# A two-layer hybrid transformer on one core: the low part of the score products over 128 rows, and a softmax tile's transpositions, scores and values each in one run

## The chip, the cores and the metric

The kernel runs on 1 of the 8 cores of one Trainium2 chip. A core has TensorE (PE: matrix products; its weight loads are shown apart as PEld), VectorE (DVE), ScalarE (ACT), GpSimd (POOL) and SyncE (SP), which here issues the DMAs. The metric is the time of one execution on the device in microseconds (us). Before the change the median of 3 runs is 3375.31 us.

## The reference

Two layers work on 1024 latent tokens and 256 context tokens of width 1024. In each layer one input projection feeds three groups of heads: gated linear attention, neighbourhood attention on a 16 x 64 grid (6 heads), and sliding-window attention (6 query heads, 2 key heads). An output projection and a SwiGLU feed-forward block follow. The change concerns the two softmax groups:

```
# neighbourhood attention: 8 x 32 keys around a block of queries, with a bias, and all context keys
s_loc = jnp.einsum('brnqhd,brnkchd->bhrnqkc', q_blk, k_blk) * scale + bias
s_ctx = jnp.einsum('brnqhd,blhd->bhrnql', q_blk, kc) * scale
p = jax.nn.softmax(jnp.concatenate([s_loc, s_ctx], axis=-1), axis=-1)
o = einsum(p_loc, v_blk) + einsum(p_ctx, vc)
# sliding window: 3 blocks of 128 keys, all context keys, and one sink logit for each head
p = jax.nn.softmax(jnp.concatenate([s_loc, s_ctx, s_sink], axis=-1), axis=-1)[without the sink]
o = einsum(p_loc, vb) + einsum(p_ctx, vc)
```

In the first layer the context tokens are queries too, over the context keys alone.

## The kernel before, in words

All work is in fp32. For products that need more exactness, an operand is split into a high part, rounded to the fast format fp32r, and a low part, the rest. The big projections take three fp32r products for each pair of operands (high x high, high x low, low x high).

**Softmax tiles.** A tile is 128 queries of two heads ("pair"). A head has 64 channels, so the scores have 64 rows to sum over. `make_q` (L785) loads the high part of a head's queries into rows 0 to 63 and the low part into rows 64 to 127. `make_k` (L791) loads the high part of the keys into both halves of k1, and the low part into rows 0 to 63 of k2 alone. `qk` (L798) adds two products in one PSUM bank: all 128 rows of q with k1 (L799: high x high plus low x high), and 64 rows of q with k2 (L800: high x low). q is the stationary operand and is loaded for every product.

`softmax_pair` (L803) makes the scores of a tile: for each head a product pair with the 256 context keys (bank sc) and one with up to 384 local keys (bank sl). DVE evicts both into the tile P and takes the extreme of each row (L809 for sc, L815 for sl, whose custom instruction also adds the bias or the mask); ACT then takes the exponential and its row sums in place (L819). `pv_pair` (L831) makes the values. P has up to five chunks of 128 keys. For two chunks at a time, four PE transpositions (two chunks, two heads; L838) fill a bank ptp, which DVE (first two chunks, L844) or ACT (the others, L842) copies to a buffer pT. Then four products (L847) of 128 rows and 64 columns add to the output, where each head takes one half of the columns of PE. `normalised` (L853) follows after the last tile of a group of up to four: reciprocal of the sums, copied 64 wide (bc, L865), transposed on PE (rrt, L869), evicted by ACT (ys, L875) and multiplied with the output (L876), which SP then stores.

**Order.** `pipeline` (L880) sets the order in which the code issues this: the scores of a tile, then the values of the tile before it (depth 1). A scheduler then places the instructions of each engine by priority and by a timeline of its own; each engine runs its list strictly in that order. Buffers come from pools that rotate: PSUM banks in three pools (p_a 2, p_b 3, p_c 3; sc and sl are in p_c), six buffers w2 for pT, bc and ys, and for P four buffers p5 in the sliding window and four each of wh and wl in neighbourhood attention.

**Stages.** In layer 0 the sliding window (swa) is interleaved with the last projections (nqk, nvp) and with the modulation vectors for later (bank mod, L301, weights wm by DMA). Neighbourhood attention (na) follows: three pairs of heads, each with loads of q, k1, k2, values (vw) and bias tables (gt, gm; POOL adds them, L1022), and with two halves of four tiles. Layer 0 has 30 tiles in each group, layer 1 has 24. The output projection (op) and the feed-forward block (pg, pu, pd) come after.

Of the kernel before, what the change touches and what calls it, by code (L numbers as in the profile page):

```python
# [11 lines left out]
F32 = mybir.dt.float32  # L12
# [3 lines left out]
ALU = mybir.AluOpType  # L16
# [71 lines left out]
def hybrid_layers(ctx: ExitStack, tc: tile.TileContext, A, K, out):  # L88
    nc = tc.nc
    V, S, G, PE, SY = nc.vector, nc.scalar, nc.gpsimd, nc.tensor, nc.sync  # L90
# [36 lines left out]
    def p_b(s):  # L127
        return ps.tile([128, 512], F32, tag="pb", name=nm(s), bufs=3)
# [10 lines left out]
    def small(s, w=1):  # L139
        return sm.tile([128, w], F32, tag=f"s{w}", name=nm(s), bufs=7)  # L140
# [53 lines left out]
    yD = [[dr.tile([D, n], F32, name=f"yD{l}_{o}") for (o, n) in (B0, B1, BC)] for l in range(DEPTH)]  # L194
# [61 lines left out]
    def rev(t, off, dims):  # L256
        return bass.AP(tensor=t.tensor, offset=t.offset + off, ap=[list(t.ap[0])] + dims)
# [527 lines left out]
    def make_q(src, r0, nn, alloc):  # L785
        q = alloc("q", F32R)
        for i in range(2):
            SY.dma_start(q[64 * i:64 * i + 64, 0:nn].bitcast(F32), src[i][r0:r0 + 64, 0:nn])
        return q

    def make_k(src, r0, alloc):  # L791
        k1, k2 = alloc("k1", F32R), alloc("k2", F32R)
        for i in range(2):
            SY.dma_start(k1[64 * i:64 * i + 64].bitcast(F32), src[0][r0:r0 + 64, :])
        SY.dma_start(k2[0:64].bitcast(F32), src[1][r0:r0 + 64, :])
        return k1, k2

    def qk(dst, q, k, qs, ks):  # L798
        PE.matmul(dst, qs(q), ks(k[0]), start=True, stop=False)  # L799
        PE.matmul(dst, qs(q)[0:64], ks(k[1])[0:64], start=False, stop=True)  # L800


    def softmax_pair(nl, emit_loc, emit_ctx, bias, nsk, m, sums):  # L803
# [24 lines left out]
        else:  # L828
            S.activation(dst, src, AF.Copy)

    def pv_pair(pr, nck, vfun, op, bank):  # L831
        c = 0
        while c < nck:
            w = min(2, nck - c)
            tp = bank("ptp")
            for cc in range(w):
                for i in range(2):
                    PE.transpose(tp[:, (cc * 2 + i) * 128:(cc * 2 + i + 1) * 128],  # L838
                                 pr[i][:, (c + cc) * 128:(c + cc + 1) * 128], ident)
            pT = t_w2("pT")  # L840
            if c >= 2:
                S.activation(pT[:, :w * 256], tp[:, :w * 256], AF.Copy)  # L842
            else:
                V.tensor_copy(pT[:, :w * 256], tp[:, :w * 256])  # L844
            for cc in range(w):
                for i in range(2):
                    PE.matmul(op[64 * i:64 * i + 64], vfun(i, c + cc),  # L847
                              pT[:, (cc * 2 + i) * 128:(cc * 2 + i + 1) * 128],
                              start=(c + cc == 0), stop=(c + cc == nck - 1), tile_position=(0, 64 * i))
            c += w  # L850


    def normalised(op, mins, sums, nt, nsk=None, grid=False):  # L853
        bc = t_w2("bc")
        n = 128 * nt
        rr = small("rr", 8)
        if nsk is not None:
            e = small("e", 8)
            V.tensor_tensor(e[:, :2 * nt].rearrange("p (j h) -> p j h", h=2),
                            mins[:, :2 * nt].rearrange("p (j h) -> p j h", h=2),  # L860
                            nsk.unsqueeze(1).to_broadcast([128, nt, 2]), ALU.subtract)
            S.activation(e[:, :2 * nt], e[:, :2 * nt], AF.Exp)
            V.tensor_tensor(sums[:, :2 * nt], sums[:, :2 * nt], e[:, :2 * nt], ALU.add)
        V.reciprocal(rr[:, :2 * nt], sums[:, :2 * nt])
        V.tensor_copy(bc[:, :n].rearrange("p (j c) -> p j c", c=64),  # L865
                      rr[:, :2 * nt].unsqueeze(2).to_broadcast([128, 2 * nt, 64]))
        rt = p_b("rrt")
        for j in range(nt):
            PE.transpose(rt[:, 128 * j:128 * j + 128], bc[:, 128 * j:128 * j + 128], ident)  # L869
        ys = t_w2("ys")  # L870
        dst, num, den = ys[:, :n], op[:, :n], rt[:, :n]
        if grid:
            dst = dst.rearrange("p (r n c) -> p r n c", n=4, c=16)
            num, den = [t.rearrange("p (n r c) -> p r n c", r=8, c=16) for t in (num, den)]
        S.activation(dst, den, AF.Copy)  # L875
        V.tensor_tensor(dst, dst, num, ALU.mult)  # L876
        return ys


    def pipeline(tiles, depth):  # L880
        late = []
        for scores, values in tiles:
            scores()
            late.append(values)
            if len(late) > depth:
                late.pop(0)()
            yield
        for values in late:
            values()

    def swa_mix(l, ctx_out):
        nn = N if ctx_out else T
        vsw = t_s("vsw")
        SY.dma_start(vsw.rearrange("p (t e) -> p t e", e=128), vswD[l].rearrange("(t p) e -> p t e", p=128))
        ks = [make_k(swD[l][2 * g + 1], 64, t_s) for g in range(2)]

        def tile(pair, qs, nsk, b, i, jt, nt, box):
            lo, hi = (max(i - 1, 0), min(i + 2, 8)) if i < 8 else (0, 0)
            m0 = 128 * (lo - i + 1) if i < 8 else 0
            cks = list(range(lo, hi)) + [8, 9]  # L900
            nl = 128 * (hi - lo)

            def qsl(x):
                return x[:, i * 128:(i + 1) * 128]

            def scores():
                if jt == 0:
                    box["m"], box["sums"] = small("m", 8), small("sums", 8)
                box[jt] = softmax_pair(
                    nl,  # L910
                    lambda a, dst: qk(dst, qs[a], ks[pair[a][0]], qsl, lambda x: x[:, lo * 128:hi * 128]),
                    lambda a, dst: qk(dst, qs[a], ks[pair[a][0]], qsl, lambda x: x[:, T:N]),
                    lambda a: swam[:, m0:m0 + nl], nsk,
                    box["m"][:, 2 * jt:2 * jt + 2], box["sums"][:, 2 * jt:2 * jt + 2])

            def vf(a, c):
                o = cks[c] * 128 + 64 * pair[a][0]
                return vsw[:, o:o + 64]

            def values():  # L920
                if jt == 0:
                    box["op"] = p_b("swo")
                op = box["op"]
                pv_pair(box[jt], len(cks), vf, op[:, 128 * jt:128 * jt + 128], p_b)
                if jt == nt - 1:
                    ys = normalised(op, box["m"], box["sums"], nt, nsk)
                    for a in range(2):
                        r0 = 640 + 64 * (3 * pair[a][0] + pair[a][1])
                        SY.dma_start(yD[l][b][r0:r0 + 64, :], ys[64 * a:64 * a + 64, :128 * nt])
            return scores, values  # L930
# [10 lines left out]
        return pipeline(tiles(), 1)  # L941

    CS = (0, 8, 24, 32)
    PAT = (0, 1, 1, 2)
# [2 lines left out]
    def na_mix(l, ctx_out):  # L947
# [4 lines left out]
        def tile(p, qs, ks, half, n, nt, gms, vw, box):  # L952
            ctx_tile = half == 2
# [18 lines left out]
            def vf(a, c):  # L972
# [3 lines left out]
                o = (c if ctx_tile else c - 3) * 384 + 128 * p + 64 * a  # L976
                return vctx[:, o:o + 64]

            def values():
                if n == 0:  # L980
                    box["op"] = p_b("nao")
                op = box["op"]
                pv_pair(box[n], 2 if ctx_tile else 5, vf, op[:, n * 128:(n + 1) * 128],
                        p_a)
                if n == nt - 1:
                    ys = normalised(op, box["m"], box["sums"], nt, grid=not ctx_tile)
                    SY.dma_start(yD[l][half][256 + 128 * p:384 + 128 * p, :], ys[:, :128 * nt])
            return scores, values

        def tiles():  # L990
            for p in range(3):
# [22 lines left out]
                for half in range(2):  # L1014
# [13 lines left out]
        return pipeline(tiles(), 1)  # L1028


    def out_proj(l, blks):
# [218 lines left out]
```

## Time and profile before

| what | value |
|---|---|
| median of 3 runs | 3375.31 us (3372.78 to 3394.1) |
| the profiled execution | 3358.87 us; its span 3357.1 us |
| TensorE clock granted, mean | 0.98 |
| read from HBM, written | 251.25 MB, 60.91 MB |
| instructions | 49501 |

The profile shows one execution. Its sums give the busy time of each engine, with PE busy 97% of the span; the chain is the work that ended last, followed back from the end. A group of instructions is shown by line, engine, operation and the names of what it writes and reads (`sc<-k,q`), with its shape: `64*128 64x256` is a stationary operand of 64 rows and 128 columns, and 256 columns that move past it. An fp32 product whose operands aren't in the fast format is shown as two matmuls (so four value products of a chunk pair appear as x8). The ends of matmuls are modelled, so the time that one costs is read from its start to the start of the next. Durations in a group's row are in ns, window bounds in us from the start of the span.

### The profile page before, as it was taken

To read this page: it belongs to the slowest core of one execution; us is meant where nothing else is said; L and a number is where in the kernel's file an instruction comes from. 1 tells how busy PE (TensorE), PEld (TensorE's weight loads), DVE (VectorE), ACT (ScalarE), POOL (GpSimd) and SP (SyncE) were. 2 spreads that over 40 slices of the span, in tenths; PEclk is the share of its full clock that TensorE was granted. 3 is DMA by queue.
4 is the path that set the end of the run, shared out by engine and by line. 5 is a ranking of instruction groups with operands and counts; after the bars stand their busy time and mean duration, and the time that the engine had idled before them with its cause. 6 is when DMAs were issued, how large, how long until landed. Compare 5 with 4: busy or idle time off the path is not lost.

```text
span 3357.1 us, 49501 instructions
## 1 busy us (share of the span) xinstructions
PE 3262.3 (97%) x19732; PEld 2668.1 (79%) x19732; DVE 1821.2 (54%) x3585; ACT 931.1 (28%) x1738; POOL 756.6 (23%) x633
## 2 busy tenths in 40 slices
PE   7999999999999999999999899999999999999998
PEld 5888876667888888888888798876668788888887
DVE  3255444556576666666556635435556555555555
ACT  4332133455321111111112332224554211111112
POOL 1011100120179889885000101010211000000000
PEclk9999999999999999999999998999999999999999
DMA  7243447454222222221111223344444111111111
GB/s 245 77 150 104 130 134 191 136 150 143 88 66 76 82 76 82 79 76 59 43 38 33 85 90 110 111 135 122 130 129 139 51 48 47 51 45 51 51 51 57
DMA packets 316208, 315.39 MB, mean 94 GB/s; under 512 B 62445, under 2 KB 246473, under 8 KB 315977
## 3 DMA queue, kind: packets, MB, share of 16 engines
q1 hardware_dynamic: 314824, 308.04, 30.4%
q10 hardware_dynamic: 1152, 4.19, 0.3%
q8 instruction: 155, 2.54, 0.3%
q14 instruction: 77, 0.62, 0.1%
HBM read 251.25 MB, written 60.91 MB: 93 GB/s over the span
## 4 chain that ended last, share of the span: by engine, by line
PE 92%; DVE 3%; DMA 2%; ACT 1%; issue 1%; POOL 0%; SPq 0%; ACTq 0%; DVEq 0%; POOLq 0%
PE pg L432 16%; PE pd L1093 16%; PE pu L432 16%; PE op L432 6%; PE nqk L432 5%; PE gp L432 5%; PE ptp L838 4%; PE swp L439 4%; PE nvp L439 3%; PE nao L847 2%; PE sl L800 2%; PE swo L847 2%; PE sc L800 2%; PE gvp L439 2%; PE sl L799 1%; PE op L670 1%
## 5 line engine op out<-in xcount | busy, mean ns | idle before, releaser
L1094 DVE SCALAR_TENSOR_TENSOR x<-pd,modT,x 128x512 f32<-128x512 f32 (+1 forms) x888 | 561.6, 686 | 385.1 <-PE pd L1093 382.9
L432 PE MATMUL pg<-yh,wch 128*128 128x512 f32 (+1 forms) x888 | 327.3, 369 | 5.2 <-ACT yh L414 3.3
L432 PE MATMUL pg<-yl,wch 128*128 128x512 f32 (+1 forms) x888 | 326.7, 368 | 0.0
L432 PE MATMUL pg<-yh,wcl 128*128 128x512 f32 (+1 forms) x888 | 326.1, 367 | 0.0
L432 PE MATMUL pu<-yh,wch 128*128 128x512 f32 (+1 forms) x888 | 325.8, 367 | 0.0
L432 PE MATMUL pu<-yh,wcl 128*128 128x512 f32 (+1 forms) x888 | 325.8, 367 | 0.0
L432 PE MATMUL pu<-yl,wch 128*128 128x512 f32 (+1 forms) x888 | 325.7, 367 | 0.0
L1093 PE MATMUL pd<-al,wdh 128*128 128x512 f32 (+1 forms) x888 | 323.3, 368 | 0.0
L1093 PE MATMUL pd<-ah,wdl 128*128 128x512 f32 (+1 forms) x888 | 323.1, 368 | 0.0
L232 DVE TENSOR_TENSOR wcl<-wr,wch 128x1024 fp32r<-128x1024 f32 x142 | 194.7, 1372 | 218.6 <-ACT wch L230 214.4
L336 POOL TENSOR_SCALAR mp<-wm,sT 128x512 f32<-128x512 f32 x168 | 284.2, 1705 | 41.8 <-DVE mpart L343 34.9
L230 ACT ACTIVATE wch<-wr 128x1024 fp32r<-128x1024 f32 x144 | 152.6, 1060 | 477.1 <-PE pd L1093 174.9
L1093 PE MATMUL pd<-ah,wdh 128*128 128x512 f32 (+1 forms) x888 | 261.2, 370 | 0.6 <-ACT ah L1086 0.3
L337 POOL TENSOR_TENSOR macc<-macc,mp 128x512 f32<-128x512 f32 x168 | 224.4, 1365 | 0.0
L819 ACT ACTIVATE P<-P,m 128x640 f32<-128x640 f32 (+2 forms) x216 | 168.1, 778 | 131.1 <-DVE m L815 102.5
L432 PEld LDWEIGHTS pg<-yh,wch 128*128 128x128 f32 x888 | 168.2, 189 | 33.7 <-ACT yh L414 3.6
L1093 PEld LDWEIGHTS pd<-al,wdh 128*128 128x128 f32 x888 | 168.2, 189 | 28.3
L432 PEld LDWEIGHTS pu<-yl,wch 128*128 128x128 f32 x888 | 167.6, 189 | 28.4
L432 PEld LDWEIGHTS pu<-yh,wch 128*128 128x128 f32 x888 | 167.7, 189 | 27.9 <-DVE a L1084 0.2
L432 PEld LDWEIGHTS pg<-yl,wch 128*128 128x128 f32 x888 | 168.3, 189 | 26.9 <-DVE yl L415 0.4
L1093 PEld LDWEIGHTS pd<-ah,wdl 128*128 128x128 f32 x888 | 168.2, 189 | 26.8
L432 PEld LDWEIGHTS pu<-yh,wcl 128*128 128x128 f32 x888 | 167.6, 189 | 27.3
(290 smaller groups left out, 6402.2 us busy)
## 6 DMA issues: line engine op xcount, KB each, us to landing
wm<-in_w_mod_dram SPq DMA_DIRECT2D x96, 256.0 KB
wr<-in_w_gate_dram SPq DMA_DIRECT2D x44, 512.0 KB
wr<-in_w_up_dram SPq DMA_DIRECT2D x44, 512.0 KB
wd<-in_w_down_dram SPq DMA_DIRECT2D x44, 512.0 KB
wm<-in_w_mod_dram SPq DMA_DIRECT2D x40, 512.0 KB
wr<-in_w_out_dram SPq DMA_DIRECT2D x32, 512.0 KB
gm<-in_const_nam_dram SPq DMA_DIRECT2D x24, 576.0 KB
wr<-in_w_in_dram SPq DMA_DIRECT2D x24, 512.0 KB
```

The source lines that it names most:

```text
L230: S.activation(h, raw, AF.Copy)
L232: engine.tensor_tensor(l, raw, h.bitcast(F32), ALU.subtract)
L336: G.tensor_scalar(t, r, sT[:, k, v:v + 1], None, ALU.mult)
L337: G.tensor_tensor(acc[v], acc[v], t, ALU.add)
L432: PE.matmul(pt[:, :n], a[:, k, :], b[k][:, o:o + n], start=(k == 0 and i == 0), stop=(k == KD - 1 and i == 2))
L439: PE.matmul(pt[:, :n], a[k][:, t * 128:(t + 1) * 128], b[:, k % 2, c0:c0 + n], start=(k == 0 and i == 0), stop=(k == KD - 1 and i == 2))
L800: PE.matmul(dst, qs(q)[0:64], ks(k[1])[0:64], start=False, stop=True)
L819: exps[:] = [S.activation(P, P, AF.Exp, bias=m[:, i:i + 1], scale=-1.0, accum_out=sums[:, i:i + 1])]
L838: PE.transpose(tp[:, (cc * 2 + i) * 128:(cc * 2 + i + 1) * 128], pr[i][:, (c + cc) * 128:(c + cc + 1) * 128], ident)
L847: PE.matmul(op[64 * i:64 * i + 64], vfun(i, c + cc), pT[:, (cc * 2 + i) * 128:(cc * 2 + i + 1) * 128], start=(c + cc == 0), stop=(c + cc = ...
L1093: PE.matmul(pd[:, :n], w[:, m * 128:(m + 1) * 128], b[:, :n], start=(i == 0), stop=(i == 2))
L1094: V.scalar_tensor_tensor(x[m][:, o:o + n], pd[:, :n], modT[l][:, v, 40 + m:41 + m], x[m][:, o:o + n], ALU.mult, ALU.add)
```

## The change

Three things change, all in the softmax groups.

1. `make_k` loads the low part of the keys into both halves of k2, and `qk` takes all 128 rows of q with it. The sum gains the product low x low. Each call issues one DMA more.
2. `pv_pair` is split. `turn_pair` makes all transpositions and copies of a tile (up to three pT), and `pv_pair` then all its value products. In neighbourhood attention the third bank comes from p_b rather than p_a. `normalised` is split too: `denominators` (everything up to ys) is called after the transpositions of a group's last tile, and `normalised` (the multiplication) after its values.
3. `pipeline` keeps two tiles instead of one. A step issues the transpositions of the oldest tile, then the scores of the tile two ahead, then the values of the oldest.

```diff
@@ make_k, qk
         for i in range(2):
             SY.dma_start(k1[64 * i:64 * i + 64].bitcast(F32), src[0][r0:r0 + 64, :])
-        SY.dma_start(k2[0:64].bitcast(F32), src[1][r0:r0 + 64, :])
+            SY.dma_start(k2[64 * i:64 * i + 64].bitcast(F32), src[1][r0:r0 + 64, :])
...
-        PE.matmul(dst, qs(q)[0:64], ks(k[1])[0:64], start=False, stop=True)
+        PE.matmul(dst, qs(q), ks(k[1]), start=False, stop=True)
@@ pv_pair
-    def pv_pair(pr, nck, vfun, op, bank):
-        c = 0
-        while c < nck:
+    def turn_pair(pr, nck, banks):
+        res = []
+        for g, c in enumerate(range(0, nck, 2)):
             w = min(2, nck - c)
-            tp = bank("ptp")
+            tp = banks[g]("ptp")
...
+            res.append(pT)
+        return res
+
+    def pv_pair(pT, nck, vfun, op):
+        for c in range(nck):
+            for i in range(2):
+                o = ((c % 2) * 2 + i) * 128
+                PE.matmul(op[64 * i:64 * i + 64], vfun(i, c), pT[c // 2][:, o:o + 128],
+                          start=(c == 0), stop=(c == nck - 1), tile_position=(0, 64 * i))
@@ pipeline
-        for scores, values in tiles:
-            scores()
-            late.append(values)
-            if len(late) > depth:
-                late.pop(0)()
-            yield
-        for values in late:
-            values()
+        def step(scores=None):
+            if scores is None or len(late) == 2:
+                turns, values = late.pop(0)
+                turns()
+                if scores:
+                    scores()
+                values()
+            else:
+                scores()
+        for scores, turns, values in tiles:
+            step(scores)
+            late.append((turns, values))
+            yield
+        while late:
+            step()
@@ swa_mix, na_mix
+            def turns():
+                box[jt] = turn_pair(box[jt], len(cks), (p_b, p_b, p_b))
+                if jt == nt - 1:
+                    box["ys"] = denominators(box["m"], box["sums"], nt, nsk)
...
+                box[n] = turn_pair(box[n], 2 if ctx_tile else 5, (p_a, p_a, p_b))
```

What the scheduler makes of it on PE is shown at neighbourhood attention in layer 1, in the middle of a group. Names carry the number of their buffer; a tile's two P belong to its two heads, ptp are the transpositions, nao the values. Before, over a little more than one chunk pair:

```order
L847 MATMUL nao_22707<-pT_22809,vw_22580 64x128 x4
L838 MATMUL ptp_22826<-ident,P_22738 128x128
L838 MATMUL ptp_22826<-ident,P_22739 128x128
L799 MATMUL sl_22915<-k_4142_22569,q_22563 128x384
L800 MATMUL sl_22915<-k_4143_22570,q_22563 128x384
L799 MATMUL sc_22906<-k_4144_22574,q_22566 128x256
L800 MATMUL sc_22906<-k_4145_22575,q_22566 128x256
L799 MATMUL sl_22919<-k_4144_22574,q_22566 128x384
L800 MATMUL sl_22919<-k_4145_22575,q_22566 128x384
L847 MATMUL nao_22707<-pT_22820,vw_22580 64x128 x2
L847 MATMUL nao_22707<-pT_22820,vctx_22115 64x128 x2
```

And after, at the same place, from the last of a tile's transpositions to the end of its values:

```order
L838 MATMUL ptp_22953<-ident,P_22851 128x128
L799 MATMUL sc_22958<-k_4136_22552,q_22546 128x256
L800 MATMUL sc_22958<-k_4137_22553,q_22546 128x256
L799 MATMUL sl_22967<-k_4136_22552,q_22546 128x384
L800 MATMUL sl_22967<-k_4137_22553,q_22546 128x384
L852 MATMUL nao_22977<-pT_22944,vw_22564 64x128 x4
L838 MATMUL ptp_22988<-ident,P_22909 128x128
L852 MATMUL nao_22977<-pT_22951,vw_22564 64x128 x2
L852 MATMUL nao_22977<-pT_22951,vctx_22125 64x128 x2
L838 MATMUL ptp_22995<-ident,P_22909 128x128
L852 MATMUL nao_22977<-pT_22956,vctx_22125 64x128 x2
```

Seven of a tile's ten transpositions now stand together, with the second head's of the last chunk at their end; the other three, the first of each bank, stand between the values of the tile before. So the values of a tile are cut into three pieces there, as before.

On DVE, at the same place, in order: L809 and L815 of one head, then the other's, and the copy L844 of the tile that is turned (ISA is the custom instruction of L815, the row with m alone reads its extreme). Before:

```order
L809 TENSOR_SCALAR P_23444,m_23331<-sc_23443 128x256
L815 ISA P_23444,m_23331<-sl_23452,gm_23321,m_23331 128x384
L815 ISA m_23331 128x1
L844 COPY pT_23357<-ptp_23352 128x512
L809 TENSOR_SCALAR P_23445,m_23331<-sc_23443 128x256
L815 ISA P_23445,m_23331<-sl_23456,gm_23326,m_23331 128x384
```

After:

```order
L809 TENSOR_SCALAR P_22959,m_22847<-sc_22958 128x256
L815 ISA P_22959,m_22847<-sl_22967,gm_22818,m_22847 128x384
L815 ISA m_22847 128x1
L809 TENSOR_SCALAR P_22960,m_22847<-sc_22958 128x256
L844 COPY pT_22993<-ptp_22988 128x512
L815 ISA P_22960,m_22847<-sl_22971,gm_22823,m_22847 128x384
```

The copy has moved behind the second head's L809, and stands ahead of that head's L815.

On SP, the loads of one pair of heads for neighbourhood attention in layer 1 (4037, 4039 and 4137 are k2). Before:

```order
L794 DMA k_4036_22123<-naD_1_144 64x1280 x2
L795 DMA k_4037_22124<-naD_1_144 64x1280
L794 DMA k_4038_22128<-naD_1_144 64x1280 x2
L795 DMA k_4039_22129<-naD_1_144 64x1280
L999 DMA vw_22133<-vD_136 128x1x128 x2
```

After:

```order
L788 DMA q_22549<-naD_2_145 64x1024 x2
L794 DMA k_4136_22552<-naD_3_146 64x1280
L795 DMA k_4137_22553<-naD_3_146 64x1280
L794 DMA k_4136_22552<-naD_3_146 64x1280
L795 DMA k_4137_22553<-naD_3_146 64x1280
L794 DMA k_4138_22558<-naD_3_146 64x1280
```

k2 is now loaded in two halves like k1, so each pair of heads issues eight key loads instead of six ahead of its vw.

More of the change, by code (lines that the diff above doesn't have):

```diff
@@ L844, in pv_pair, with denominators @@
                 V.tensor_copy(pT[:, :w * 256], tp[:, :w * 256])
[L845 to L853, printed above, removed]
+            res.append(pT)
[6 more added lines that the diff above has]
+                          start=(c == 0), stop=(c == nck - 1), tile_position=(0, 64 * i))
+    def denominators(mins, sums, nt, nsk=None, grid=False):
         bc = t_w2("bc")
@@ L870, in normalised, with pipeline @@
         ys = t_w2("ys")
-        dst, num, den = ys[:, :n], op[:, :n], rt[:, :n]
+        dst, den = ys[:, :n], rt[:, :n]
         if grid:
             dst = dst.rearrange("p (r n c) -> p r n c", n=4, c=16)
-            num, den = [t.rearrange("p (n r c) -> p r n c", r=8, c=16) for t in (num, den)]
+            den = den.rearrange("p (n r c) -> p r n c", r=8, c=16)
         S.activation(dst, den, AF.Copy)
+        return ys
+    def normalised(ys, op, nt, grid=False):
+        n = 128 * nt
+        dst, num = ys[:, :n], op[:, :n]
+        if grid:
+            dst = dst.rearrange("p (r n c) -> p r n c", n=4, c=16)
+            num = num.rearrange("p (n r c) -> p r n c", r=8, c=16)
         V.tensor_tensor(dst, dst, num, ALU.mult)
-        return ys
-    def pipeline(tiles, depth):
+    def pipeline(tiles):
         late = []
-        for scores, values in tiles:
-            scores()
-            late.append(values)
-            if len(late) > depth:
-                late.pop(0)()
+        def step(scores=None):
[10 more added lines that the diff above has]
+            late.append((turns, values))
             yield
-        for values in late:
-            values()
+        while late:
+            step()
     def swa_mix(l, ctx_out):
@@ L923, in values @@
                 op = box["op"]
-                pv_pair(box[jt], len(cks), vf, op[:, 128 * jt:128 * jt + 128], p_b)
+                pv_pair(box[jt], len(cks), vf, op[:, 128 * jt:128 * jt + 128])
                 if jt == nt - 1:
-                    ys = normalised(op, box["m"], box["sums"], nt, nsk)
+                    ys = box["ys"]
+                    normalised(ys, op, nt)
                     for a in range(2):
@@ L929, in values @@
                         SY.dma_start(yD[l][b][r0:r0 + 64, :], ys[64 * a:64 * a + 64, :128 * nt])
-            return scores, values
+            return scores, turns, values
         def tiles():
@@ L940, in tiles @@
                         yield tile(pair, qs, nsk, b, i, jt, len(grp), box)
-        return pipeline(tiles(), 1)
+        return pipeline(tiles())
     CS = (0, 8, 24, 32)
@@ L977, in vf, with turns @@
                 return vctx[:, o:o + 64]
+            def turns():
+                box[n] = turn_pair(box[n], 2 if ctx_tile else 5, (p_a, p_a, p_b))
+                if n == nt - 1:
+                    box["ys"] = denominators(box["m"], box["sums"], nt, grid=not ctx_tile)
             def values():
@@ L982, in values @@
                 op = box["op"]
-                pv_pair(box[n], 2 if ctx_tile else 5, vf, op[:, n * 128:(n + 1) * 128],
-                        p_a)
+                pv_pair(box[n], 2 if ctx_tile else 5, vf, op[:, n * 128:(n + 1) * 128])
                 if n == nt - 1:
-                    ys = normalised(op, box["m"], box["sums"], nt, grid=not ctx_tile)
-                    SY.dma_start(yD[l][half][256 + 128 * p:384 + 128 * p, :], ys[:, :128 * nt])
-            return scores, values
+                    normalised(box["ys"], op, nt, grid=not ctx_tile)
+                    SY.dma_start(yD[l][half][256 + 128 * p:384 + 128 * p, :], box["ys"][:, :128 * nt])
+            return scores, turns, values
         def tiles():
@@ L1027, in tiles @@
                         yield tile(p, qs, ks, half, n, 4, gms, vw, box)
-        return pipeline(tiles(), 1)
+        return pipeline(tiles())
     def out_proj(l, blks):
```

## The prediction

> **What bounds the kernel now.** I read the page first: busy shares and the chain that ended last.
>
> ```profile
> PE 3262.3 (97%) x19732; PEld 2668.1 (79%) x19732; DVE 1821.2 (54%) x3585; ACT 931.1 (28%) x1738; POOL 756.6 (23%) x633
> PE 92%; DVE 3%; DMA 2%; ACT 1%; issue 1%; POOL 0%; SPq 0%; ACTq 0%; DVEq 0%; POOLq 0%
> ```
>
> TensorE is busy almost throughout and carries 92% of the chain. A change that takes TensorE time away is therefore worth that time, as long as nothing else fills it. Next come the busy sums of the four stretches in which the softmax groups run: sliding window, then neighbourhood attention, in layer 0 and in layer 1 (columns: length; busy of PE, weight loads, DVE, ACT, POOL with counts; granted clock, DMA share, GB/s).
>
> ```profile
> 450.00:667.00 217.00, 208.70 (x1497) 143.57 (x1498) 102.19 (x346) 80.74 (x196) 11.83 (x12) 0.94 0.51 143
> 667.00:811.00 144.00, 139.91 (x1012) 91.53 (x1009) 81.72 (x256) 77.42 (x173) 23.19 (x24) 1.00 0.46 128
> 2253.00:2390.00 137.00, 135.18 (x936) 89.77 (x934) 76.59 (x249) 66.04 (x152) 11.78 (x12) 1.00 0.46 125
> 2390.00:2518.00 128.00, 123.87 (x906) 81.08 (x905) 71.37 (x221) 69.42 (x149) 23.35 (x24) 1.00 0.48 133
> ```
>
> PE idles 8.3 + 4.1 + 1.8 + 4.1 = 18.3 us in these 626 us. But a busy PE need not be streaming, because the ends of matmuls are modelled. So I read starts, in the order of time, in one stretch of layer 1's neighbourhood attention (start, time, instruction):
>
> ```profile
> 2420.49 0.66 PE L838 MATMUL ptp<-ident,P 128*128 128x128 f32 x4
> 2420.90 0.36 PE L799 MATMUL sc<-k,q 128*128 128x256 f32 x1
> 2421.19 0.38 PE L800 MATMUL sc<-k,q 64*128 64x256 f32 x1
> 2421.50 0.44 PE L799 MATMUL sl<-k,q 128*128 128x384 f32 x1
> 2421.87 0.44 PE L800 MATMUL sl<-k,q 64*128 64x384 f32 x1
> 2422.25 0.44 PE L847 MATMUL nao<-pT,vctx 128*64 128x128 f32 x4
> 2422.62 0.66 PE L838 MATMUL ptp<-ident,P 128*128 128x128 f32 x4
> ```
>
> Start to start, a product of 256 columns takes 0.29 (first) and 0.31 (second), one of 384 columns 0.37 and 0.38. The projections run the same sizes with 128 rows on both sides, one of them behind transpositions, one between runs of 64 columns:
>
> ```profile
> 2246.44 0.49 PE L838 MATMUL ptp<-ident,P 128*128 128x128 f32 x3
> 2246.68 0.36 PE L432 MATMUL nqk<-yl,wch 128*128 128x256 f32 x1
> 2246.88 0.28 PE L432 MATMUL nqk<-yh,wcl 128*128 128x256 f32 x1
> 2247.00 0.40 PE L432 MATMUL nqk<-yh,wch 128*128 128x512 f32 x1
> ...
> 2132.20 0.33 PE L439 MATMUL nvp<-wth,yl 128*128 128x384 f32 x1
> 2132.38 0.34 PE L439 MATMUL nvp<-wth,yh 128*128 128x384 f32 x1
> 2132.65 1.09 PE L670 MATMUL op<-am,gv 128*64 128x128 f32 x14
> 2133.66 0.44 PE L439 MATMUL nvp<-wtl,yh 128*128 128x384 f32 x1
> 2133.94 0.33 PE L439 MATMUL nvp<-wth,yl 128*128 128x384 f32 x1
> 2134.11 0.34 PE L439 MATMUL nvp<-wth,yh 128*128 128x384 f32 x1
> ```
>
> Among their own kind 256 columns take 0.12 (2246.88 to 2247.00) and 384 take 0.17 (2133.94 to 2134.11). The first one behind transpositions takes 0.20, so 0.08 more. The last one before a run of 64 columns takes 0.27 (2132.38 to 2132.65), 0.10 more; the first behind such a run 0.28, 0.11 more. So a change of shape costs about 0.1 between 128x128 and 128x64, and about 0.19 wherever 64 rows stand on either side.
>
> **The change, part 1: 128 rows in the second product.** The products touched (the first products are as many):
>
> ```profile
> L800 PE MATMUL sc<-k,q 64*128 64x256 f32 x216 | 83.1, 385 | 0.0
> L800 PE MATMUL sl<-k,q 64*128 64x384 f32 x168 | 75.5, 450 | 0.0
> L800 PE MATMUL sl<-k,q 64*128 64x256 f32 x24 | 9.1, 381 | 0.0
> ```
>
> That is 408 second products. In the program's order of before I counted their neighbours:
> - Into it. 233 first products stand behind a transposition or a value run: 0.29 now (2420.90 to 2421.19), 0.20 then; 0.09 x 233 = 21 us. 175 stand behind another product: 0.37 now, 0.17 then (the same 0.19 to 0.20 for 256 columns); 0.195 x 175 = 34 us.
> - Out of it. 228 are followed by a 128x128 instruction: 0.31 now (2421.19 to 2421.50), 0.12 then; 0.19 x 228 = 43 us. 180 are followed by a value run: 0.38 now (2421.87 to 2422.25), 0.27 then, since the change to 64 columns stays; 0.10 to 0.11 x 180 = 19 us.
> - 62 transpositions stand directly behind a second product. The first of a run behind a change of shape takes about 0.055 more (four take 0.41 up to 2420.90; three take 0.24 at 2246.44, so 0.11 each with 0.03 for the last): 3 us.
>
> Sum 21 + 34 + 43 + 19 + 3 = 120 us. Nothing hides this on PE; it lies on the path.
>
> [...]
>
> **Part 2: the order.** Said in words, each tile's values become one run. In the program they don't: the order has 272 exits from value runs before and 276 after. Transpositions directly ahead of a value run go from 66 to 141 (+75 x 0.10 = +7), second products there from 180 to 114 (-66 x 0.10 = -7), score products directly behind a value run from 27 to 79 (+52 x 0.11 = +6), transpositions there from 234 to 176 (-58 x 0.055 = -3). Sum +3 us: by itself the new order saves PE nothing. Its worth is cover, which I cost by one steady stretch of tiles:
>
> ```profile
> 2396.00:2498.00 102.00, 102.00 (x716) 66.55 (x711) 57.57 (x190) 53.88 (x121) 20.66 (x22) 1.00 0.45 124
> L844 DVE COPY pT<-ptp 128x512 f32<-128x512 f32 x18 | 12.4, 691 | 9.2 <-PE ptp L838 9.0
> L815 DVE CUSTOM_DVE_ANT_0 P<-sl,gm,m 128x384 f32<-128x384 f32 x39 | 24.0, 616 | 11.2 <-PE sl L800 8.6 <-issue 0.6 <-POOL gm L1022 0.4
> L809 DVE TENSOR_SCALAR_CACHE_REDUCE P<-sc 128x256 f32<-128x256 f32 x40 | 16.9, 423 | 24.1 <-PE sc L800 20.2 <-PE ptp L838 3.9
> L819 ACT ACTIVATE P<-P,m 128x640 f32<-128x640 f32 x40 | 33.0, 825 | 14.4 <-DVE m L815 14.3
> ...
> 2421.18 0.69 DVE L844 COPY pT<-ptp 128x512 f32<-128x512 f32 x1 [0.30 <-PE ptp L838]
> ```
>
> 18 tiles (one L844 copy each) take 102 us: per tile PE 5.67, DVE 57.57 / 18 = 3.2, ACT 3.0. A tile has four second products; by the four cases above it loses about 1.25, so PE needs 4.4 and stays the longest, DVE at 73%. Where can it wait? In the new order the seven transpositions of a tile stand behind a second product whose L809 (0.42) goes ahead of the L844 copy (0.69) on DVE. The copy of 2421.18 began 0.28 us after the step behind its last transposition (2420.90). With the same 0.28, L809 runs from 0.40 to 0.82 after the start of that second product, and the copy from 0.82 to 1.5. PE reaches the values after 0.12 + 7 x 0.11 + 0.32 + 0.44 = 1.65 us. That is enough by 0.1 to 0.2, not by more. Queued behind that copy are L815 and, through it, the exponential; both are for a tile whose transpositions come a whole tile later. Waits have a lower bound of -18 us (today's idle goes) and an upper one of a half copy per tile, 108 x 0.35 = +38. I take +8, since the walk through one tile came out just covered.
>
> Denominators move from behind the values to ahead of them: the same reciprocal, copy, four transpositions and eviction per group, 0 us, covered by the values. They hold two of the six w2 buffers longer; three pT and these two make five, so the next tile's first copy still has one.
>
> **Part 3: transfers.** The 16 make_k calls issue one DMA more each, 327 KB, on SP's queue:
>
> ```profile
> L795 SPq DMA_DIRECT2D k<-naD x12: 444/544/594, 539.6 to 2420.1; - x12
> L795 SPq DMA_DIRECT2D k<-swD x4: 451/499/547, 361.9 to 2176.6; - x4
> 544.00:616.00 72.00, 65.46 (x541) 42.35 (x537) 33.16 (x118) 25.34 (x61) 0.00 (x0) 0.84 0.80 210
> L301 PE MATMUL mod<-wm,sT 128*32 128x128 f32 x512 | 26.4, 299 | 6.5 <-DMA wm<-in_w_mod_dram 6.5
> ```
>
> Issue is 16 x 0.54 = 9 us of a queue, ahead of vw and gt loads there; 0 where loads run a head pair ahead. One place isn't covered: from 544 to 616 layer 0's modulation weights share the DMA engines (80% busy, 210 GB/s) with the first two head pairs, and PE waits for wm. Some nine tiles fall there, about 10 us of the gain, and four extra loads of 0.33 MB take 6 us at 210 GB/s. Bounds 0 to 16; I take 8, because PE is still busy 65 of the 72 us.
>
> **Sum.** -120 + 3 + 8 + 8 = -101 us. The profiled execution took 3358.9 (span 3357.1), the median of the runs is 3375.3, 16 more, with the same program; so 3258 for a profiled execution and 3274 for the median, which I forecast.
>
> **Rivals.**
> - Waits fill part of what PE gives up: DVE and ACT become the pace in half of the tiles. For it: the margin of 0.1 to 0.2 above, and swa's two free banks. Against: 73% load. 108 x 0.45 = 49 us back: 3323.
> - The second product isn't slow for its 64 rows (but, say, for accumulating onto a bank just written). Only the order is left, +3, waits as now: 3378. Against: the projections accumulate onto one bank at 0.12.
> - The weight load of a 128-row product isn't hidden behind its neighbour: 816 score products x 0.11, the step of a transposition with its load, = 90 us back: 3364. Against: the 0.12 of the projections. [...]
> - Slower: the tile two ahead isn't ahead. The sliding window has four P buffers, two tiles' worth, so L809 of a new tile waits for the last transposition of the old one. If that puts L809, L815, the exponential and a copy (0.42 + 0.62 + 0.82 + 0.69, with the hops over 3 us) in PE's way with 1.5 us left open in each of 108 tiles, that is +162: 3428 with the other terms (-120 + 3 + 8 + 162). It decides from 0.95 us a tile. Against: the new order has a full tile of values and transpositions between.
>
> **Chances.** Forecast (3245 to 3305): 0.74. Better than 3245: 0.03. Partly filled: 0.13. Load not hidden: 0.04. Not the rows: 0.03. Slower: 0.03. The range 3240 to 3325 holds the forecast and the better part of the second case. A measurement of this kernel tells about 1% from no change, so faster means under 3341: 0.88; within 1%: 0.09; slower: 0.03.
>
> **What would show it.** Part 1: L800 becomes 128*128; first and second sc start 0.12 to 0.20 apart and sl 0.17 to 0.28; if they stay at 0.3, a rival of the product is right. Part 2: value runs still cut by single transpositions; the tile at 4.3 to 4.7 us instead of 5.67, with PE waits for pT under 0.3 a tile. Waits of PE on L844 or L842 above 0.5 a tile, or on L809, mean the first or the last rival. Part 3: mod waiting more for wm before 620. The prediction is wrong if the stretches from 450 to 811 and 2253 to 2518 don't shrink by about 50 us each, or if the clock there falls below the 0.94 to 1.00 granted now.

## The result, and the profile after

| | before | after |
|---|---|---|
| median of 4 runs | 3374.05 us (3359.21 to 3394.1) | 3289.41 us (3285.48 to 3292.5) |
| the profiled execution | 3358.87 us | 3290.15 us |
| its span, mean granted clock | 3357.1 us, 0.980 | 3288.3 us, 0.977 |

The ratio is 0.9745, with a 95% interval from 0.9693 to 0.9797. The time forecast was 3274, so it came out 15 us above, inside the range. The sum had said 101 us less: the medians differ by 85, the profiled executions by 69 (3290 where 3258 was forecast). In the changed kernel's profile the value products stand at L852, bc at L868, rrt at L872 and ys at L878; swo are the values of the sliding window.

The busy shares and the chain that ended last, of the changed kernel:

```profile
PE 3160.9 (96%) x19732; PEld 2649.7 (81%) x19732; DVE 1812.4 (55%) x3585; ACT 929.3 (28%) x1738; POOL 755.3 (23%) x633
PE 89%; DMA 4%; DVE 4%; ACT 1%; issue 1%; SPq 0%; POOL 0%; ACTq 0%; DVEq 0%; POOLq 0%
```

PE lost 101 us of busy time. That this equals the forecast's sum is chance: the sum's terms for PE, -120 and +3, make 117, and the other 16 are for waits and transfers. The span shrank by 69 only, and DMA and DVE now stand in the chain with 4% each, from 2% and 3%. Where that lies is seen in the two softmax stretches, from the first score to the first product of the output projection. First the kernel before, layer 0 and layer 1 (columns as in the prediction: length; busy of PE, weight loads, DVE, ACT, POOL; clock, DMA share, GB/s), then the changed one:

```profile
429.00:810.00 381.00, 369.15 (x2612) 250.03 (x2611) 192.33 (x628) 163.78 (x378) 37.55 (x38) 0.97 0.50 142
2233.00:2519.00 286.00, 279.50 (x1934) 185.99 (x1933) 155.53 (x496) 141.40 (x312) 35.13 (x36) 1.00 0.45 126
```

```profile
434.00:780.00 346.00, 318.20 (x2609) 240.43 (x2609) 187.31 (x628) 162.74 (x378) 37.72 (x38) 0.96 0.58 163
2210.00:2452.00 242.00, 231.21 (x1934) 179.98 (x1932) 148.61 (x495) 141.02 (x311) 35.26 (x36) 0.97 0.55 154
```

PE's busy time falls by 51 and 48 us, but the stretches shrink by 35 and 44, for PE's idle time grows from 11.9 to 27.8 us in layer 0 and from 6.5 to 10.8 in layer 1. The clock falls a little too, 0.97 to 0.96 and 1.00 to 0.97. (That is 79 us together. The rest of the span became 10 us longer, ahead of the stretches and between them, where PE runs code that the change does not touch; one execution does not tell that from scatter.)

The instructions themselves, a tile of layer 1's neighbourhood attention after the change (start, time, instruction):

```profile
2384.27 0.36 PE L799 MATMUL sc<-k,q 128*128 128x256 f32 x1
2384.47 0.28 PE L800 MATMUL sc<-k,q 128*128 128x256 f32 x1
2384.59 0.35 PE L799 MATMUL sl<-k,q 128*128 128x384 f32 x1
2384.78 0.34 PE L800 MATMUL sl<-k,q 128*128 128x384 f32 x1
2384.95 0.27 PE L838 MATMUL ptp<-ident,P 128*128 128x128 f32 x1
2385.16 0.66 PE L852 MATMUL nao<-pT,vw 128*64 128x128 f32 x8
2385.75 0.33 PE L838 MATMUL ptp<-ident,P 128*128 128x128 f32 x1
2386.01 0.44 PE L852 MATMUL nao<-pT,vw 128*64 128x128 f32 x4
```

L800 has 128 rows, and the steps are 0.20 behind a transposition, then 0.12, 0.19 and 0.17, where there were 0.29 to 0.38. The value run is cut by a single transposition at 2385.75. The steady part (18 tiles, counted by the L844 copies, as before):

```profile
2353.00:2436.00 83.00, 82.89 (x735) 63.41 (x733) 52.58 (x181) 52.59 (x115) 21.01 (x22) 1.00 0.58 164
L844 DVE COPY pT<-ptp 128x512 f32<-128x512 f32 x18 | 12.4, 688 | 0.8 <-PE ptp L838 0.8
```

82.89 / 18 = 4.6 us of PE a tile, from 5.67. So the tiles became as short as expected where nothing stops them. What stops them is in PE's waits, layer 0 (434 to 780) and then layer 1 (2210 to 2452); columns: what waited and for what, us in sum, times, longest:

```profile
PE mod L301 <- DMA wm<-in_w_mod_dram: 17.1, 4, 6.8
PE ptp L838 <- ACT pT L842: 4.7, 2, 4.2
PE nao L852 <- DVE pT L844: 2.9, 2, 2.0
...
PE swo L852 <- ACT pT L842: 7.0, 2, 6.0
PE nao L852 <- DVE pT L844: 2.3, 2, 2.0
```

Before, PE waited 6.5 us for wm, and for pT no more than 1.1 us at a time (layer 0, then the longest for pT, in layer 1):

```profile
PE mod L301 <- DMA wm<-in_w_mod_dram: 6.5, 5, 1.9
PE nao L847 <- ACT pT L842: 1.7, 2, 1.1
```

Two waits for pT are long now, 4.2 and 6.0 us. The second one, in the order of time: SyncE's queue, ScalarE, TensorE.

```profile
2275.13 0.45 SPq L794 DMA_DIRECT2D k<-naD  x1
2276.19 0.45 SPq L795 DMA_DIRECT2D k<-naD  x1
2277.78 1.83 SPq L954 DMA_DIRECT2D yD<-ys  x2
2280.69 11.79 SPq L1028 DMA_DIRECT2D vw<-vD  x11
```

```profile
2279.81 0.60 ACT L842 ACTIVATE pT<-ptp 128x512 f32<-128x512 f32 x1 [0.62 <-PE ptp L838]
2287.43 0.38 ACT L842 ACTIVATE pT<-ptp 128x256 f32<-128x256 f32 x1 [7.03 <-DMA yD<-ys]
```

```profile
2281.23 0.66 PE L852 MATMUL swo<-pT,vsw 128*64 128x128 f32 x8
2287.87 0.69 PE L852 MATMUL swo<-pT,vsw 128*64 128x128 f32 x2 [5.98 <-ACT pT L842]
2288.49 0.69 PE L799 MATMUL sl<-k,q 128*128 128x384 f32 x1
2288.97 0.53 PE L800 MATMUL sl<-k,q 128*128 128x384 f32 x1
```

The last copy of a tile (256 columns, 2287.43) doesn't wait for its transpositions; it waits for the two y stores issued by 2279.61. Copy and store are tied by memory: pT, bc and ys all come from the six w2 buffers, and here a ys buffer came free only when its store had landed (ACT waited the 7.03 us above for it). Those stores stand in SyncE's queue behind eight key loads of 320 KB (L794 and L795, from 2267.75 on), and the DMA engines are busy all that time:

```profile
2267.00:2281.00 14.00, 14.00 (x128) 10.67 (x126) 10.74 (x37) 8.69 (x20) 0.00 (x0) 1.00 1.04 226
```

The packets in the trace show the order: the 512 of 5120 bytes, the rows of the keys, run until 2286, and the 128 of 2048 bytes, the rows of ys, start only at 2282.7 and go on to 2287.

In all ACT waits 15.7 us for y stores in the changed kernel, four times; in the kernel before no copy to pT waits for one.

### The profile page after: what moved, and what is told of

Read it like the earlier page. It is cut to its first block, busy times and chain, and to the rows that moved or that the text cites. A ratio compares the mean times of both kernels' runs of the same rounds, so it can differ in the third digit from the quotient of the medians.

```text
span 3288.3 us, 49560 instructions
## 1 busy us (share of the span) xinstructions
PE 3160.9 (96%) x19732; PEld 2649.7 (81%) x19732; DVE 1812.4 (55%) x3585; ACT 929.3 (28%) x1738; POOL 755.3 (23%) x633
## 4 chain that ended last, share of the span: by engine, by line
PE 89%; DMA 4%; DVE 4%; ACT 1%; issue 1%; SPq 0%; POOL 0%; ACTq 0%; DVEq 0%; POOLq 0%
PE pg L432 16%; PE pu L432 16%; PE pd L1122 16%; PE op L432 6%; PE nqk L432 5%; PE gp L432 5%; PE swp L439 4%; PE ptp L838 4%; PE nvp L439 3%; PE swo L852 2%; PE nao L852 2%; PE gvp L439 2%; PE op L670 1%; DMA wm<-in_w_mod_dram 1%; PE sl L799 1%
## 5 line engine op out<-in xcount | busy, mean ns | idle before, releaser
L432 PEld LDWEIGHTS pg<-yh,wcl 128*128 128x128 f32 x888 | 167.9, 189 | 26.6
```

The source lines that it names most:

```text
L432: PE.matmul(pt[:, :n], a[:, k, :], b[k][:, o:o + n], start=(k == 0 and i == 0), stop=(k == KD - 1 and i == 2))
```

## The experiments

Twelve runs, each also timed in five rounds against the kernel before, whose medians there were 3372.2, 3366.7, 3364.3 and 3365.7 us. An interval of a ratio is some 0.3% (10 us) to either side.

### Each part alone

`rows_only`, part 1 in the old order:

```diff
         for i in range(2):
             SY.dma_start(k1[64 * i:64 * i + 64].bitcast(F32), src[0][r0:r0 + 64, :])
-        SY.dma_start(k2[0:64].bitcast(F32), src[1][r0:r0 + 64, :])
+            SY.dma_start(k2[64 * i:64 * i + 64].bitcast(F32), src[1][r0:r0 + 64, :])
...
-        PE.matmul(dst, qs(q)[0:64], ks(k[1])[0:64], start=False, stop=True)
+        PE.matmul(dst, qs(q), ks(k[1]), start=False, stop=True)
```

> Part 1 alone: 128 rows in the second product and the extra loads, with the order and the pipeline of before. Theory (the 128 rows are the whole gain of TensorE, the order saves it nothing): score steps fall as in the changed kernel (first to second product 0.12 to 0.20, 408 second products, about 119 us of PE by the step table), the wait for wm in layer 0 grows by some 10 us as there, and the waits for pT behind a y store are absent or smaller, since sums and reciprocals are again taken behind the values: 3260 to 3290 us, level with the changed kernel or up to 30 below it. Rival (the new order is the cover that part 1 needs): in the old order PE waits for pT copies and exponentials in most tiles, at least 0.3 us in each of 108: 3310 or more, and the sum of PE's waits for L842 and L844 above 35 us.

`order_only`, the changed kernel with these lines taken back:

> Part 2 alone: turns, scores of a tile two ahead and values in one run each, with 64 rows in the second product and no extra load. Theory (the order by itself saves PE nothing): +3 to +15 us of PE steps and up to 15 us of waits behind the y stores: 3374 to 3404, that is, the same as before or a little slower. Rival (the order brings part of the measured gain): 3350 or less.

Part 1 alone: 3281.1 us, ratio 0.9737 (0.9708 to 0.9767), 8 us below both parts together. Part 2 alone: 3379.4, ratio 1.0024 (1.0003 to 1.0044). So all of the gain is the rows', and the order brings none; both times lie where the theory had put them. PE's waits for L842 and L844 came to 19 us with the rows alone, not 35. But the theory had put the waits for y stores down to the new order, and there they are in the old one as well, while the order alone has none:

```profile
ACT pT L842 <- DMA yD<-ys: 11.2, 3, 5.5
DVE pT L844 <- DMA yD<-ys: 4.8, 2, 4.3
```

(the run of the rows alone). They come with faster tiles, not with where the denominators stand.

### The extra loads

`no_extra_load`: the changed kernel, the second product reading the first key tile, whose 128 rows are loaded anyway; `ys_ev_no_load` the same on top of `ys_ev` (its one line stands in the next part).

```diff
-            SY.dma_start(k2[64 * i:64 * i + 64].bitcast(F32), src[1][r0:r0 + 64, :])
+        SY.dma_start(k2[0:64].bitcast(F32), src[1][r0:r0 + 64, :])
...
-        PE.matmul(dst, qs(q), ks(k[1]), start=False, stop=True)
+        PE.matmul(dst, qs(q), ks(k[0]), start=False, stop=True)
```

> The changed kernel, but the second product reads the first key tile (all 128 rows of it) instead of the second one, which is loaded as in before with 64 rows: the products' sizes are those of the changed kernel, the 16 extra loads are left out, and so is the low part of the keys. Theory (the extra loads cost about 10 us in layer 0, where the modulation weights share the DMA engines, and lengthen the queue ahead of the y store in layer 1): PE's wait for wm falls from 17 back to 6 to 9 us, 8 to 20 us less than the changed kernel: 3270 to 3281. Rival (PE comes earlier to the same wm, whatever else is loaded): the wait for wm stays at 14 to 20 us and the time within 5 us of the changed kernel, 3284 to 3294.

Measured 3290.7: the rival. The wait for wm is as long without the extra loads:

```profile
PE mod L301 <- DMA wm<-in_w_mod_dram: 17.9, 9, 5.0
```

A y store held a copy here too, 8.8 us on DVE, so the test was repeated where none does:

> The kernel with ys in the ev buffers (3272), and in it the second product reads the first key tile as in the earlier run, so that the 16 extra loads and the low part of the keys are left out. This repeats the test of the extra loads where no y store holds the copies. Theory (the loads themselves cost next to nothing; PE comes earlier to wm, whatever is loaded): wm waits of 15 to 22 us in layer 0 as with the loads, 3266 to 3277. Rival (the loads do cost their 6 to 10 us, and the stall behind the y store hid it in the earlier run): 3256 to 3265.

3274.1 us, against 3272.3 with the loads, and 19.9 us of wait for wm. The loads cost nothing that can be measured, and the wait for wm does not come from them. That PE is simply at wm sooner is what remains of the two explanations; no run tests it by itself.

### The buffers of ys

`ys_ev`, one line of the changed kernel:

```diff
-        ys = t_w2("ys")
+        ys = t_ev("ys")
```

> The changed kernel with the tile ys of the denominators in another pool (the three ev buffers) than the turned P tiles (six w2 buffers). Theory (the copies pT at L842 wait for a w2 buffer that a y store frees only when it has landed, behind key and value loads): the two waits of ACT for the y store, 4.9 and 7.0 us, are gone, and with them 4.2 and 6.0 us of PE and the half clock behind them: 3271 to 3281. Rival (what holds the copies is the busy DMA queue, and the wait only moves to a load or to the ev buffers): within 5 us of the changed kernel, with as long a wait elsewhere in the same two places.

3272.3 us, 17 below the changed kernel; no copy to pT waits for a y store any more, and layer 1's stretch has no wait of PE over 2.0 us. The same line in the old order with the rows:

> Part 1 alone in the old order, and ys in the ev buffers. Theory (the order is worth nothing either way, once no copy is held by a y store): the 16.0 us that ACT and DVE waited for y stores in the run of part 1 alone go down to under 3, and the time to 3264 to 3278, level with the new order with ys in ev (3272). Rival (the new order is cover worth having): 3283 or more, with PE waits for L842 and L844 growing to above 25 us in sum.

3262.9 us, a little better than expected, and again some 9 us below the new order. The waits of the copies for y stores are gone there as well, but one came back under another name: the projections that run beside the sliding window use the ev buffers too.

```profile
DVE lo L713 <- DMA yD<-ys: 11.6, 2, 9.7
```

Beside it ACT's `hi` waits 10.9 us for an ev buffer from its own store, and behind these PE waits 8.8 us for a copy on ACT. So the line moves the shortage to a pool where it hurts less; it doesn't end it.

### The wait for wm

`ys_ev_mod`, with one step of the modulation for each of the projections instead of one for two, and `ys_ev_poolq`, with its loads on GpSimd's queue (L296), each on top of `ys_ev`:

```diff
-        proj = merge(proj, rest, 2, 1)
+        proj = merge(proj, rest, 1, 1)
```

```diff
-                SY.dma_start(rv, A["w_mod"][l, 256 * q:256 * q + 256, 512 * u:512 * u + 512]
+                G.dma_start(rv, A["w_mod"][l, 256 * q:256 * q + 256, 512 * u:512 * u + 512]
```

> The kernel with ys in the ev buffers, and the modulation of layer 0 taken one step for each step of the projections instead of one for two, so that 7 instead of 16 of its 32 wm loads are left when the first values of the sliding window run. Theory (the waits for wm in the softmax stretch come from 16 loads of 512 KB that now have less time): the wait for wm in the stretch from 434 to 660 falls from 21 to under 10 us and 8 to 25 us of time go with it: 3247 to 3264. Rival (the loads only collide with others further ahead, in the projections, or the order there gets worse): 3268 to 3290, with the wm wait at another place.

> The kernel with ys in the ev buffers, and the 32 wm loads of layer 0's modulation issued from GpSimd's queue instead of SyncE's. Theory A (wm is late because its issue stands in SP's queue behind y stores that wait for ys, and behind key and value loads): the wait for wm falls below 8 us, 3252 to 3264. Theory B (the DMA engines are the limit, 0.75 to 0.87 busy in these slices, or the two buffers): the wait stays at 15 us or more, 3268 to 3280.

The first: 3278.5, the rival. No wait for wm is left, and the wait stands at the head of the neighbourhood attention instead, for its keys; the clock is at one half for 20 us there, 13 of them behind the wait:

```profile
PE sc L799 <- DMA k<-naD: 14.1, 2, 12.5
```

The second: 3261.0, 11 us less, but with 14.2 us of wait for wm left, from 20.9 (`ys_ev`, then `ys_ev_poolq`):

```profile
PE mod L301 <- DMA wm<-in_w_mod_dram: 20.9, 5, 6.8
PE mod L301 <- DMA wm<-in_w_mod_dram: 14.2, 5, 7.1
```

It lies between the theories: the time is theory A's, the remaining wait B's. Part of the wait is the issue in SyncE's queue; what the rest is, the DMA engines or the two buffers, was not tried.

### The parts with the obstacles out of the way

The old order with the rows and both edits, and the kernel before with both edits:

> Part 1 alone in the old order, with ys in the ev buffers and the wm loads on GpSimd's queue; beside the earlier run of the new order with the same two edits (3261). Theory (the order as the program has it saves PE nothing, 424 us of softmax steps in both): within 10 us of it, 3251 to 3268, and about 105 to 120 us under before, the whole of the forecast's first term. Rival (the new order is worth its cover): 3271 or more. Rival (the new order costs): 3248 or less.

> The kernel before, 64 rows in the second product, with the two edits found on the way: ys in the ev buffers and the wm loads on GpSimd's queue. It differs from the run of part 1 alone with these edits (3253) by the rows and the extra loads only. Theory (the rows are worth the forecast's first term, about 120 us, and the two edits remove waits that only a faster PE meets): in before no copy waits for a y store and PE waits 6.5 us for wm, so the edits give 0 to 10 us: 3354 to 3368, the rows then 101 to 115. Rival (the edits are worth 15 us or more by themselves, and the rows less than 95): 3345 or less.

3252.8 (ratio 0.9659, 0.9634 to 0.9685), the lowest of all medians, and 3363.1 (1.0003, 0.9973 to 1.0033). Both as the theory said: the edits show no gain in the kernel before, and the rows are worth 3363.1 - 3252.8 = 110 us. The obstacles are not all gone, though. PE's longest wait in the two stretches, in the kernel before with both edits and then with the rows:

```profile
PE swo L847 <- ACT pT L842: 4.1, 1, 4.1
PE swo L847 <- ACT pT L842: 10.3, 1, 10.3
```

In the second, ACT itself waits 12.4 us for an ev buffer for `hi`, which an earlier store still holds, and the copy stands behind it. With 7.6 us for wm, PE's idle time in the two stretches is 31 us, against 12 without the rows.

### Whole value runs

The code asks for one value run a tile, the program has 265. Both runs bind instructions to the order of the code, on top of `ys_ev_poolq` (3261.0): `v_keep` the value products as below, `vtq_keep` in the same way also the transpositions of L838 and the score products of L799 and L800.

```diff
-                PE.matmul(op[64 * i:64 * i + 64], vfun(i, c), pT[c // 2][:, o:o + 128],
-                          start=(c == 0), stop=(c == nck - 1), tile_position=(0, 64 * i))
+                tc.keep_in_program_order(PE.matmul(op[64 * i:64 * i + 64], vfun(i, c), pT[c // 2][:, o:o + 128],
+                          start=(c == 0), stop=(c == nck - 1), tile_position=(0, 64 * i)))
```

> The new order with ys in the ev buffers and wm on GpSimd's queue (3261), and the value products bound to the order in which the code issues them among themselves: in the program 172 value runs instead of 265. Theory (the order saves nothing because the value runs are cut; each cut costs its change of shape): the step table gives 395 instead of 424 us for the softmax steps, -29 us: 3228 to 3245. Rival (a bound order takes the cover away and PE waits as much for pT as it gains): 3250 or more, with PE waits for L842 and L844 above 25 us in sum.

> The same as the run before it, but transpositions and score products are bound as well, so that a tile's transpositions, the scores of the tile two ahead and the values stand as the change's words say: 108 value runs, no transposition inside them. Theory (cuts are what is left to save; DVE at 3.2 and ACT at 3.0 us a tile still fit under PE): the step table gives 375 instead of 424 us, -49, of which up to 25 may go to waits: 3212 to 3237. Rival (with PE near 3.8 us a tile DVE and the copies become the pace, and the bound order lets nothing else step in): 3245 or more, PE waits for L842, L844 and L809 above 45 us in sum.

`v_keep`: 3257.2, 4 us less, within the scatter: the time lies where the rival had it, but without the rival's waits for pT. Added up over all starts of the two stretches (no step counted over 0.45 us), the value products' steps fell from 154.5 to 142.2 us, but all softmax steps only from 446.5 to 437.6 instead of by 29; waits for L842 and L844 did not grow. The step table overrates such a rearrangement. Counting steps at half the granted clock as half, all softmax steps fall from 439 to 426, by 13. In this profiled execution more of them fell on the half clock, which takes back 5; and PE's idle time in the stretches grew by 6 us (26 to 32), with more waits for L809, L815 and bc. Together that explains about all of what is missing.

`vtq_keep`: 3309.1, 48 us more: the second run's rival. PE waits, first layer 0, then layer 1:

```profile
PE sc L799 <- DVE P L809: 19.6, 32, 2.3
PE rrt L872 <- DVE bc L868: 16.0, 15, 4.4
...
PE sc L799 <- DVE P L809: 26.0, 44, 1.0
PE rrt L872 <- DVE bc L868: 10.0, 12, 1.6
```

Not the copies pT but L809 and the reciprocals' bc hold it, 72 us together. Here the scheduler's freedom to place what it reckons to be ready, a single transposition inside a value run among it, was worth more than whole runs.

## Why the prediction was right, and where it was not

The runs make a chain from before to after in which each link differs in one thing:

| from | to | what differs | us |
|---|---|---|---|
| 3363.1 (before, both edits) | 3252.8 | the rows | -110 |
| 3252.8 | 3261.0 | the order | +8 |
| 3261.0 | 3272.3 | wm on SyncE's queue | +11 |
| 3272.3 | 3289.4 | ys among the w2 buffers | +17 |

The kernels were timed in several sessions, beside medians of before from 3364 to 3374. By the ratios to before the links are -116, +6, +10 and +13 us, and each is uncertain by 10 us or more. In sum they make -74 (-87 by the ratios), not the forecast's -101.

- **The first term, -120 for the rows,** was right in mechanism, and some 10% too large. The softmax steps, added up as above, fall from 558.7 to 444.3 us between the first two kernels of the table, by 114, and from 553.9 in before to 453.9 in `rows_only`, by 100. The executions profiled differ in how much ran at half the granted clock; with steps at half clock counted as half, the two pairs give 104 and 109. Of these the first products make 46 and 48 us, where the prediction had 21 + 34 = 55, and the second ones 56 and 59, where it had 62. No weight load shows in the steps: in the tile above the second sc product, at 2384.47, is 0.12 ahead of the next one, and its load of 0.19 us had begun at 2384.35, 0.08 after the start of the first product. The times of the two rivals on the product, 3378 and 3364, did not come.
- **+3 for the order** was right as PE time: the steps are 457.3 in the changed kernel and 453.9 with the rows alone; 2 to 3 us in the other two pairs as well. With 64 rows the order costs more, 570.9 in `order_only` against 553.9 in before: the -7 that the prediction takes off for second products is there only with 128 rows. As time the new order lost 8, 9 and 8 us in three pairs (with ys in w2, with ys in ev, with both edits; 3, 5 and 6 by the ratios) and 7 with 64 rows. Each of these is hardly more than one pair can tell; that all four agree speaks for a small loss.
- **+8 for waits:** here a step failed. "They hold two of the six w2 buffers longer; three pT and these two make five, so the next tile's first copy still has one." It counted buffers as if ys were free after its multiplication. In the trace it was free when its store had landed, and the store was late behind the key loads (7.03 us of ACT's wait above). That cost 17 us (three pairs of kernels differ in that line alone, by 17, 17 and 18). The part of the step that walked through a tile was right: in `ys_ev`, where no store is in the way, PE waits 8 us in all for L842 and L844, so DVE and the copies keep up, and the rival in which they become the pace did not come about.
- **+8 for transfers:** the place was right (wm, layer 0), and so was nearly the size (11), but not the cause. The prediction put it down to "four extra loads of 0.33 MB". Without them nothing changes. What is left is PE's own gain, which brings it to wm sooner; SyncE's queue is part of why wm is not there yet (20.9 us of wait with it, 14.2 without), and the rest is open. Together the two terms for waits and transfers, 16 us, are near the 20 by which PE's idle time in the two stretches grew (18.4 to 38.6).
- **The base.** The sum started from a median of three runs, 3375.3, and medians of before over 11 to 17 runs lie at 3364 to 3372. From 3366 the same sum would have said 3265, 24 us too low. The forecast was near its number partly because the base was high, which is luck: its sum for the change itself is too large by 16 us in the medians and by 32 in the profiled executions.
- **What would show it:** steps of 0.12 to 0.20 and 0.17 to 0.28, value runs cut, a tile at 4.3 to 4.7, more wait for wm: all seen. The stretches shrank by 35 and 44 us, not by "about 50 us each", so one of the prediction's own signs of being wrong did appear, above all in layer 0; PE's busy time in them fell by 51 and 48.

## What to carry to other kernels

A matmul with 64 rows among ones with 128 cost about 0.27 us more here, its neighbours' part included (110 us over 408 of them): filling its rows with a second copy of the data was worth that, though all it adds to the sum is the product low x low. A tile that was stored belonged here to the store until that had landed (a copy waited 7.0 us for it, and ys in another pool saved 17): count its buffer through the DMA queue, and keep it out of the pool that the next compute step draws from. When an engine becomes faster, look at what it will now meet first (stores, loads two buffers ahead), and judge each such obstacle with the faster engine, since the same two edits took the changed kernel from 3289.4 to 3261.0 us and left the kernel before where it was (3363.1, ratio 1.0003).

## Not expected of the hardware

A wait of TensorE cost more than its length. From 3.6 us before the end of the 6.0 us wait (2287.9) the granted clock was one half for 10.2 us, and then full (the first two windows; the third is round the end, at 569.0, of a wait for wm of 6.8 us):

```profile
2284.30:2294.50 10.20, 6.63 (x25) 5.44 (x26) 2.41 (x6) 3.40 (x8) 0.00 (x0) 0.50 0.27 81
2294.50:2304.50 10.00, 9.90 (x94) 7.51 (x93) 6.05 (x21) 5.93 (x14) 0.00 (x0) 1.00 0.50 152
...
567.40:577.60 10.20, 8.60 (x62) 5.76 (x62) 2.47 (x8) 1.52 (x3) 0.00 (x0) 0.50 0.60 182
```

The product of 384 columns at 2288.49 above took 0.48 to the next one, instead of 0.27 to 0.28. The lengths at half clock in the softmax stretches are 3.4, 6.8 and 10.2 us, 44 us in all against 25 in the kernel before. The softmax steps in them add up to 29 and 16 us, so at half speed an estimated 6 us of the gain are lost.

How long the clock stays at one half does not follow from the wait. In the kernel before, waits of 1.9 and 1.8 us came with 13.7 and 10.2 us (the first two windows). In `before_ev_poolq` one wait of 4.1 us came with 44.4 us, while PE was busy for 41.6 of them:

```profile
569.19:582.85 13.66, 11.83 (x78) 7.82 (x82) 3.54 (x11) 2.21 (x5) 0.00 (x0) 0.50 1.01 258
606.74:616.98 10.24, 10.24 (x46) 6.00 (x47) 3.52 (x12) 2.23 (x5) 0.00 (x0) 0.50 0.70 196
...
574.24:618.61 44.37, 41.63 (x214) 26.66 (x214) 15.93 (x60) 13.32 (x35) 2.89 (x4) 0.50 0.73 193
```

So two profiled executions can differ in time at half clock without the change having a part in it. The lengths measured, 3.4, 6.8, 10.2, 13.7 and 44.4 us, are near whole multiples of 3.4. What makes the clock fall was not shown: in the 3.4 us before it fell, PE was busy for 2.5, 1.6 and 2.1 us in these three cases, and for 1.0 and 0.0 us in the two of the changed kernel.
